# Moving the convolution, gate, factor and score steps of a four-part fp32 network on one core

## The chip, the cores and the metric

The kernel runs on one core of one Trainium2 chip. Its time is the device time of one execution in microseconds; a lower one is better. The engines are named as in the profile: PE is TensorE with PEld for its weight loads, DVE is VectorE, ACT is ScalarE, POOL is GpSimd, and SP is the queue that issues the transfers of the weights.

## The reference

Two blocks follow each other over one sequence of 256 tokens with 1024 features, all in fp32. The first block is a mixer of retention and latent attention with a SwiGLU network behind it. The second block has an even layer (spatial gate and stick-breaking attention), an MLP, an odd layer (mLSTM) and an MLP. The change touches a step of the retention, the even layer and the odd layer. Cut to these:

```
def _even_mixer(h, ...):
    ...
    q = _rmsnorm_2(zb[..., :B_WIDTH].reshape(bsz, seq, B_HEADS, B_HDIM), qn_g)
    k = _rmsnorm_2(zb[..., B_WIDTH:2 * B_WIDTH].reshape(bsz, seq, B_HEADS, B_HDIM), kn_g)
    ...
    o = _stick_breaking(to_bhsd(q), to_bhsd(k), to_bhsd(v))

def _odd_mixer(h, w_in, conv_w, conv_b, i_b, f_b, on_g, w_out):
    p = h @ w_in
    qk = jax.nn.silu(_causal_conv(p[..., :n_qk], conv_w, conv_b))   # four taps
    ...
    hc = _mlstm(q, k, v, i_pre, f_pre)

# _mlstm, by chunk: logf = log_sigmoid(f_pre); bcum = cumsum(logf)
dmat = where(tril, bcum[..., :, None] - bcum[..., None, :] + li[..., None, :], -inf)
m_t = maximum(g, max(dmat, -1))
wts = exp(dmat - m_t[..., None])
s = einsum('bhtd,bhsd->bhts', qc, kc) * wts
den = sum(s, -1) + inter * einsum('bhtd,bhd->bht', qc, n_st)
h = num / maximum(abs(den), exp(-m_t))[..., None]
```

## The kernel before, in words

Activations lie with features on the partitions and the 256 tokens along the free axis. Weights stream from memory in blocks of 128 x 1024 in the order of use. Each block is split into a high part H (rounded, by ScalarE, L368) and a rest L (by VectorE, L369), and each weight tile makes three TensorE products: high with high, high with low, low with high. They go into the PSUM tiles `st`; a product over feature tiles has 256 columns (`fm`, `fm2`), one over token tiles has 512 (`nat`). These are the stream products. All small products (sums over partitions, spreads of a row over partitions, transposes, scores, outputs) go into four PSUM tiles `sd` and are called side steps.

A side step is a closure. `side` puts steps in a list of which one is issued after each so many ticks (a tick is one weight tile of 128 columns); `plan` gives each step a fixed tick; `tick` issues what is due; `drain` issues all that is left. This sets the order in which the program is written. A scheduler then orders each engine's instructions by its own estimates, so a step can move a little against the stream; products issued with the last argument of `mm` true (`follow`) keep the written order among themselves, and a step wrapped in `urgent` has priority.

In the odd layer `qk_head(h)` takes head h's two halves (a query and a key tile). For each half it applies the four taps: ScalarE makes two products (L1295, L1296), GpSimd one product (L1297, tile `cvb`) and a sum (L1298, `cva`), VectorE a product with sum (L1299) and a sum (L1300); then tanh (L1302) and a last step into `qk` (L1303). `gate_chain` makes from the gate columns the rows B (running sum), `cc`, M (running maximum) and `em` = exp(-(B + M)) (L1321, L1322), whose minimum with 1e17 GpSimd takes (L1323). `gate_cols` turns `cc` and `em` into columns by four products of four columns each; `weights(h)`, `scores(h)` and `dens` use them.

In the even layer `project` makes queries, then keys. `head_sums` sums their squares by head, `head_factor` makes the factors (`faq` for queries, L1075 to L1082), and `q_scale` spreads `faq` over the partitions by 16 products and multiplies the queries (L1098). In the retention `outs(g)` makes the output of a pair of heads.

Of the kernel before, what the change touches and what calls it, by code (L numbers as in the profile page):

```python
# [11 lines left out]
ALU = mybir.AluOpType  # L12
# [4 lines left out]
T = 256  # L17
# [220 lines left out]
class K:  # L238
# [294 lines left out]
    def mixer1(s):  # L533
        nc, ap = s.nc, s.ap
# [225 lines left out]
        def outs(g):  # L760
            def f():
                Vc = Vcs[g]
                po = s.psd().rearrange("p (q h d) -> p q h d", q=2, h=2)
                for q in range(2):
                    for i in range(2):
                        for j, (t0, n) in enumerate(KT):
                            s.mm(po[:, q, i], Ss[g, j][:n, i, q * 128:q * 128 + 128], Vc[:n, i, j], j == 0, j == 2)
                oo = on[g // 2][:, :, (g % 2) * 256:(g % 2) * 256 + 256]
                nc.scalar.copy(oo, po.rearrange("p q h d -> p q (h d)"))
                vs = s.sm(4, "vs")  # L770
                jk = s.wk(T, "w256")[:, :128]
                for q in range(2):
                    for i in range(2):
                        nc.scalar.activation(jk, po[:, q, i], AF.Square, accum_out=vs[:, 2 * q + i:2 * q + i + 1])
                cb = comb[:, :, 2 * g:2 * g + 2]
                t = s.sm(4, "gnv")
                nc.vector.tensor_scalar(t, vs, 1.0 / 128, 1e-5, ALU.mult, ALU.add)
                nc.gpsimd.tensor_tensor(t, t, s.c("mhalf", 0, 4), ALU.pow)
                for q in range(2):
                    nc.vector.tensor_scalar(cb[:, q], t[:, 2 * q:2 * q + 2], r128[:, q:q + 1], 0.5, ALU.mult, ALU.mult)  # L780
                if g < 2:
                    decay(g + 2)
            return f

        for h in range(8):
            p = s.pst()[:, :NA]
            s.fm(("w_in",), 8, (p,), H, L)
            vt = s.wk(288, "P")
            nc.gpsimd.memset(vt[:, NA:], 0.0)
            nc.vector.tensor_mul(vt[:, :NA], p, rb)  # L790
            g, i = h // 2, h % 2
            s.side([center(g, i, vt)] + ([scores(g, 1), scores(g, 2), outs(g)] if i else [stack(g), scores(g, 0)]), 2)


        cH, cL = (lambda kt: ckvH[:, kt]), (lambda kt: ckvL[:, kt])
# [244 lines left out]
    def even(s):  # L1040
# [42 lines left out]
                                            0.125 if w == "q" else 1.0, ALU.mult, ALU.mult)  # L1083
            return f

        def q_scale(g):
            def f():
                fa = fac["q"]
                pb = s.psd().rearrange("p (f n) -> p f n", f=2)
                for i in range(2):  # L1090
                    t = 2 * g + i
                    for j in range(2):
                        for e in range(2):
                            col = fa[:, 8 * j + 2 * t + e:8 * j + 2 * t + e + 1]
                            s.mm(pb[64 * e:64 * e + 64, i, 128 * j:128 * j + 128], col.to_broadcast([128, 64]), s.c("eye"),
                                 True, True, True)
                q = qr[:, 2 * g:2 * g + 2]
                nc.vector.tensor_mul(q, q, pb)  # L1098
            return f


        yH = [s.slot(10, [128, 4, T], F32R), s.slot(11, [128, 4, T], F32R)]
# [103 lines left out]
        for q in range(2):  # L1206
# [12 lines left out]


        project("q", qr, "qg")
        s.side([s.urgent(head_sums("q")), s.urgent(head_factor("q")), s.urgent(lambda: (q_scale(0)(), q_scale(1)()))], 4)
        project("k", kT, "kg")
        s.drain()
        s.plan([(2, head_sums("k")), (6, s.urgent(head_factor("k"))), (7, st_scores(0)), (11, st_scores(1)),
                (16, spatial(0)), (20, spatial(1)), (34, st_suffix(0)), (36, st_scores(2)), (48, st_suffix(1)),
                (50, st_scores(3)), (64, st_suffix(2)), (77, st_suffix(3))])

        ug = s.slot(18, [128, 4, T])
        for g in range(2):  # L1230
# [9 lines left out]
        gate(1)  # L1240
        for q in range(2):
            nc.scalar.activation(V[:, q], ps[q], AF.Copy, scale=rr[:, q:q + 1])
        s.plan([(n, st_out(i)) for i, n in enumerate((72, 75, 80, 92))], s.ticks)
        y_h = lambda kt: yH[kt // 4][:, kt % 4]
        y_l = lambda kt: yL[kt // 4][:, kt % 4]
        s.residual("ev_w_out_2", 8, y_h, y_l, 1.0, "gp0", ahead=4)
# [19 lines left out]
    def odd(s):  # L1266
# [19 lines left out]
        def qk_head(h):  # L1286
            ps = s.fm2("od_w_in_2", 8, H, L)
            a = s.wk(2 * 259).rearrange("p (f n) -> p f n", f=2)
            nc.gpsimd.memset(a[:, :, 0:3], 0.0)
            nc.vector.tensor_mul(a[:, :, 3:], ps, s.b2(rb))  # L1290
            for i in range(2):
                f = h + 4 * i
                w = lambda t: s.v("cw", 4 * f + t)
                y, y1, y2 = s.wk(T, "w256"), s.wk(T, "cva"), s.wk(T, "cvb")
                nc.scalar.activation(y, a[:, i, 3:259], AF.Identity, bias=s.v("cb", f), scale=w(3))  # L1295
                nc.scalar.activation(y1, a[:, i, 0:T], AF.Copy, scale=w(0))  # L1296
                nc.gpsimd.tensor_scalar(y2, a[:, i, 1:T + 1], w(1), None, ALU.mult)  # L1297
                nc.gpsimd.tensor_add(y1, y1, y2)  # L1298
                nc.vector.scalar_tensor_tensor(y, a[:, i, 2:T + 2], w(2), y, ALU.mult, ALU.add)  # L1299
                nc.vector.tensor_add(y, y, y1)  # L1300
                th = s.wk(T, "w256")
                nc.scalar.activation(th, y, AF.Tanh, scale=0.5)  # L1302
                nc.vector.scalar_tensor_tensor(qk[i][:, h], th, 1.0, y, ALU.add, ALU.mult)  # L1303


        def gate_chain():
# [12 lines left out]
            nc.vector.tensor_tensor_scan(M, cc, f2, 0.0, ALU.max, ALU.max)  # L1319

            nc.vector.tensor_add(em, B, M)  # L1321
            nc.scalar.activation(em, em, AF.Exp, scale=-1.0)  # L1322
            nc.gpsimd.tensor_scalar(em, em, 1e17, None, ALU.min)  # L1323

        def gate_cols():
            pc = s.psd()
            for j in range(2):
                s.mm(pc[:, 4 * j:4 * j + 4], cc[:, 128 * j:128 * j + 128], s.c("sel4"), True, True)
                s.mm(pc[:, 8 + 4 * j:12 + 4 * j], em[:, 128 * j:128 * j + 128], s.c("sel4"), True, True)
            nc.vector.tensor_copy(ccol, pc[:, 0:16])  # L1330
            s.split(Mr[:, 0], Mr[:, 1], M)


        def weights(h):
            def f():
                w = wt[h // 2][:, h % 2]
                pb = s.psd()[:, :T]
                for i in range(2):
                    s.mm(pb, sel4r[:, h:h + 1].to_broadcast([128, 128]), Mr[:, i], i == 0, i == 1)
# [11 lines left out]
        def scores(h):  # L1351
            def f():
                w, S = wt[h // 2][:, h % 2], sw[h // 2][:, h % 2]
                p = s.psd()[:, :384]
                s.mm(p[:, 0:256], qk[1][:, h, 0:128], qk[0][:, h], True, True, h == 3)
# [4 lines left out]
        def wait():  # L1360
            pass

        def dens():

# [65 lines left out]
        p = s.pst()[:, :T]  # L1430
        s.cols4("od_w_in_2", p, "gm1", lambda kt: s.x[:, kt, NM:])
        nc.vector.tensor_mul(gs[:, 0], p, rb)
        s.side([gate_chain, gate_cols] + [weights(h) for h in range(4)] + [scores(0)], 5)
        for h in range(1, 4):
            qk_head(h)
            s.steps += [wait, wait, scores(h)] if h == 3 else [scores(h)]
        s.steps += [wait, dens]

        V = [s.slot(6, [128, 1024]), s.slot(7, [128, 1024])]
        for cch in range(2):  # L1440
# [68 lines left out]
```

## Time and profile before

| | |
|---|---|
| median of 3 runs | 1005.91 us (1005.79 to 1007.25) |
| the profiled execution's own time | 1006.0 us |
| its span | 1004.2 us |
| busy: PE, DVE, ACT, POOL | 992.4, 686.0, 567.6, 144.5 us |
| weight transfers | 172.90 MB by one queue, 57.1% of the DMA engines' time |

The span goes from the first to the last instruction. Busy times of PE come from products whose ends are modelled and overlap; the distance from start to start tells what one costs. A tile's name is the program's, without buffer numbers: `sd<-cst,faq` is a product into `sd` whose operands are a constant and `faq`.

### The profile page before, as it was taken

The numbers are of one execution on the slowest core, as the hardware profiler recorded it, in microseconds if no ns is written. First come the engines' busy times: TensorE is split into PE (matmuls) and PEld (weight loads), VectorE is DVE, ScalarE is ACT, GpSimd is POOL, SyncE is SP. The second block draws the span as 40 slices with busy tenths as digits, with TensorE's granted clock in tenths as the row PEclk, the third lists the DMA queues.
The fourth block names the chain that finished last, engine by engine and source line by source line (L and its number), as shares of the span: only waits on it lengthen the run. The fifth ranks groups of instructions, "written<-read, shape, count | busy, mean of one in ns | idle before, by whom it ended". The sixth has DMA issues, their size and how long they took to land.

```text
span 1004.2 us, 19944 instructions
## 1 busy us (share of the span) xinstructions
PE 992.4 (99%) x8214; PEld 955.1 (95%) x8214; DVE 686.0 (68%) x941; ACT 567.6 (57%) x840; POOL 144.5 (14%) x158
## 2 busy tenths in 40 slices
PE   9999999999999999999999999999989999999998
PEld 8998889999999999998889999999978999999998
DVE  6889687477776675669767767555585577665443
ACT  7796566445545554566756665444485565555432
POOL 1633100000111111447100000011171000000000
PEclk9999999999999999999999999999998999999999
DMA  8643553466666666674346666666654466666671
GB/s 337 190 131 101 153 160 109 129 193 191 191 199 192 193 193 200 204 226 148 119 121 186 189 193 193 190 196 197 187 151 142 114 187 191 198 195 190 204 207 53
DMA packets 49515, 176.73 MB, mean 176 GB/s; under 512 B 5456, under 2 KB 6736, under 8 KB 49424
## 3 DMA queue, kind: packets, MB, share of 16 engines
q1 hardware_dynamic: 47808, 172.90, 57.1%
q8 instruction: 64, 1.05, 0.5%
q0 software_dynamic: 368, 1.31, 0.4%
q10 hardware_dynamic: 1248, 1.25, 0.4%
q14 instruction: 27, 0.22, 0.1%
HBM read 174.39 MB, written 1.05 MB: 175 GB/s over the span
## 4 chain that ended last, share of the span: by engine, by line
PE 89%; DVE 3%; ACT 3%; POOL 2%; issue 1%; DMA 1%; SPq 0%; ACTq 0%; DVEq 0%; POOLq 0%
PE st L339 82%; PE sd L339 7%; DVE L L369 1%; ACT H L368 1%; PE sd L344 1%; POOL cvb L1297 1%; DMA raw<-in_wpack 1%; DVE e L757 0%; ACT w L704 0%; POOL cva L1298 0%; DVE comb L780 0%; ACT L1302 0%; DVE s L745 0%; POOL s L1218 0%; DVE vmean L725 0%
## 5 line engine op out<-in xcount | busy, mean ns | idle before, releaser
L369 DVE TENSOR_TENSOR L<-raw,H 128x1024 fp32r<-128x1024 f32 (+1 forms) x327 | 409.9, 1254 | 233.3 <-ACT H L368 231.5
L368 ACT CAST H<-raw 128x1024 fp32r<-128x1024 f32 (+1 forms) x327 | 341.8, 1047 | 350.4 <-PE st L339 266.4
L339 PE MATMUL st<-uH,H 128*128 128x256 f32 (+1 forms) x1384 | 385.7, 280 | 0.7 <-ACT H L368 0.7
L339 PE MATMUL st<-uL,H 128*128 128x256 f32 (+1 forms) x1384 | 383.8, 278 | 0.0
L339 PE MATMUL st<-uH,L 128*128 128x256 f32 (+1 forms) x1384 | 382.4, 278 | 0.6 <-DVE L L369 0.6
L339 PE MATMUL st<-s,H 128*128 128x256 f32 (+1 forms) x2004 | 343.1, 276 | 0.0
L339 PEld LDWEIGHTS st<-s,H 128*128 128x128 f32 x2004 | 301.9, 188 | 0.7 <-issue 0.5
L339 PE MATMUL st<-s,L 128*128 128x256 f32 (+1 forms) x1002 | 276.1, 276 | 0.0
L339 PEld LDWEIGHTS st<-uH,H 128*128 128x128 f32 x1384 | 259.7, 188 | 5.1 <-issue 2.4
L339 PEld LDWEIGHTS st<-uL,H 128*128 128x128 f32 x1384 | 259.9, 188 | 3.3 <-issue 2.4
L339 PEld LDWEIGHTS st<-uH,L 128*128 128x128 f32 x1384 | 258.8, 188 | 1.7 <-DVE L L369 1.0
L339 PEld LDWEIGHTS st<-s,L 128*128 128x128 f32 x1002 | 188.1, 188 | 0.2 <-issue 0.2
L339 PE MATMUL sd<-s,s 128*64 128x128 f32 (+10 forms) x280 | 46.4, 337 | 0.0
L339 PE MATMUL st<-H,uH 128*128 128x512 f32 x96 | 39.4, 410 | 0.0
L339 PE MATMUL st<-H,uL 128*128 128x512 f32 x96 | 39.4, 410 | 0.0
L339 PE MATMUL st<-L,uH 128*128 128x512 f32 x96 | 38.6, 402 | 0.0
L339 PEld LDWEIGHTS sd<-s,s 128*64 128x64 f32 (+7 forms) x280 | 30.9, 162 | 7.2 <-issue 1.5
L453 POOL TENSOR_TENSOR rstd<-rp,cst 128x2 f32<-128x2 f32 x4 | 4.7, 1179 | 209.2 <-DVE rp L452 209.2
L441 DVE TENSOR_TENSOR s<-w,s 128x512 fp32r<-128x512 f32 (+1 forms) x54 | 31.2, 580 | 0.0
L991 POOL TENSOR_TENSOR w<-w,w 128x256 f32<-128x256 f32 x22 | 16.6, 754 | 98.5 <-DVE w L990 98.5
L440 ACT CAST s<-w 128x512 fp32r<-128x512 f32 (+1 forms) x54 | 28.5, 531 | 1.1
L1258 DVE SCALAR_TENSOR_TENSOR w<-st,rb 128x512 f32<-128x512 f32 x32 | 21.8, 687 | 8.0 <-PE st L339 8.0
(282 smaller groups left out, 791.7 us busy)
## 6 DMA issues: line engine op xcount, KB each, us to landing
raw<-in_wpack SPq DMA_DIRECT2D x324, 512.0 KB, 4.0
s<-in_even POOLq DMA_DIRECT2D x2, 512.0 KB, 6.1
out_yT<-vx ACTq DMA_DIRECT2D x3, 256.0 KB, 4.9
vx<-in_vx SPq DMA_DIRECT2D x2, 272.0 KB, 5.0
s<-in_tabs SPq DMA_DIRECT2D x1, 544.0 KB, 9.5
s<-in_tabs SPq DMA_DIRECT2D x1, 448.0 KB, 8.9
cst<-in_cst SPq DMA_DIRECT2D x1, 447.5 KB, 8.2
vx<-in_vx SPq DMA_DIRECT2D x1, 408.0 KB, 7.1
```

Of the source, the lines that this page charges most:

```text
L339: i = s.nc.tensor.matmul(out, lhsT=l, rhs=r, start=start, stop=stop, skip_group_check=True)
L344: s.nc.tensor.transpose(out, a, s.c("eye", 0, n)[:n])
L368: nc.scalar.copy(H[:, c:d], raw[:, c:d])
L369: nc.vector.tensor_sub(L[:, c:d], raw[:, c:d], H[:, c:d].bitcast(F32))
L440: s.nc.scalar.copy(hi, src)
L441: s.nc.vector.tensor_sub(lo, src, hi.bitcast(F32))
L453: nc.gpsimd.tensor_tensor(out, t, s.c("mhalf", 0, n)[:out.shape[0]], ALU.pow)
L991: nc.gpsimd.tensor_mul(th, th, z[:, 1])
L1258: nc.vector.scalar_tensor_tensor(z, p, 0.0, s.b2(rb), ALU.max, ALU.mult)
L1297: nc.gpsimd.tensor_scalar(y2, a[:, i, 1:T + 1], w(1), None, ALU.mult)
```

## The change

Five things change. In the retention, an empty step is put ahead of `outs(g)`, and its products are issued with `follow`. In the even layer the steps for queries and keys get one plan with fixed ticks, counted from the start of the key projection, where before there was a list for the queries, a `drain` behind the keys, and a plan for the rest; `q_scale` becomes one step for all four tiles, at tick 37, and the four output steps get ticks that are 32 higher, since the count no longer starts anew. In the odd layer's convolution GpSimd's product goes to VectorE as a product with sum, and GpSimd makes the last sum in place of VectorE. The minimum on `em` goes from GpSimd to VectorE. The gate, weight and score steps get fixed ticks, and more of their products are issued with `follow`.

```diff
-            s.side([center(g, i, vt)] + ([scores(g, 1), scores(g, 2), outs(g)] if i else [stack(g), scores(g, 0)]), 2)
+            s.side([center(g, i, vt)] + ([scores(g, 1), scores(g, 2), lambda: None, outs(g)] if i else [stack(g), scores(g, 0)]), 2)
...
         project("q", qr, "qg")
-        s.side([s.urgent(head_sums("q")), s.urgent(head_factor("q")), s.urgent(lambda: (q_scale(0)(), q_scale(1)()))], 4)
+        s.plan([(1, s.urgent(head_sums("q"))), (3, s.urgent(head_factor("q"))), (34, head_sums("k")), (37, q_scale),
+                (39, s.urgent(head_factor("k"))), (40, st_scores(0)), (43, st_scores(1)), (48, spatial(0)), (52, spatial(1)),
+                (66, st_suffix(0)), (68, st_scores(2)), (80, st_suffix(1)), (82, st_scores(3)), (96, st_suffix(2)),
+                (109, st_suffix(3))])
         project("k", kT, "kg")
-        s.drain()
-        s.plan([(2, head_sums("k")), (6, s.urgent(head_factor("k"))), (7, st_scores(0)), (11, st_scores(1)),
...
-        s.plan([(n, st_out(i)) for i, n in enumerate((72, 75, 80, 92))], s.ticks)
+        s.plan([(n, st_out(i)) for i, n in enumerate((104, 107, 112, 124))], s.ticks)
...
-                nc.gpsimd.tensor_scalar(y2, a[:, i, 1:T + 1], w(1), None, ALU.mult)
-                nc.gpsimd.tensor_add(y1, y1, y2)
                 nc.vector.scalar_tensor_tensor(y, a[:, i, 2:T + 2], w(2), y, ALU.mult, ALU.add)
-                nc.vector.tensor_add(y, y, y1)
+                nc.vector.scalar_tensor_tensor(y1, a[:, i, 1:T + 1], w(1), y1, ALU.mult, ALU.add)
+                nc.gpsimd.tensor_add(y, y, y1)
...
-            nc.gpsimd.tensor_scalar(em, em, 1e17, None, ALU.min)
+            nc.vector.tensor_scalar_min(em, em, 1e17)
...
-        s.side([gate_chain, gate_cols] + [weights(h) for h in range(4)] + [scores(0)], 5)
+        s.plan([(2, s.urgent(gate_chain)), (40, gate_cols)] + [(43 + 3 * h, weights(h)) for h in range(4)] +
+               [(56 + 4 * h, scores(h)) for h in range(3)] + [(70, scores(3)), (77, dens)])
         for h in range(1, 4):
             qk_head(h)
-            s.steps += [wait, wait, scores(h)] if h == 3 else [scores(h)]
-        s.steps += [wait, dens]
```

What the scheduler makes of it is seen at three places. The first is VectorE in the odd layer, from the sum B + M (L1321 before, L1317 now) on. `s_8667` and `s_8668` hold the gate rows, `w_...` the halves of the convolution, `s_8671` the remainder of the split of M. Before:

```order
L1321 TENSOR_TENSOR s_8668<-s_8667,s_8668 128x256
L369 TENSOR_TENSOR L<-raw,H 128x1024
L441 TENSOR_TENSOR s_8671<-s_8668,s_8671 128x256
L1303 SCALAR_TENSOR_TENSOR s_8659<-w_9005,w_8996 128x256
L1299 SCALAR_TENSOR_TENSOR w_9008<-w_8993,vx,w_9008 128x256
```

And now:

```order
L1317 TENSOR_TENSOR s_8668<-s_8667,s_8668 128x256
L441 TENSOR_TENSOR s_8671<-s_8668,s_8671 128x256
L369 TENSOR_TENSOR L<-raw,H 128x1024
L1299 SCALAR_TENSOR_TENSOR s_8659<-w_8963,w_8956 128x256
L1294 SCALAR_TENSOR_TENSOR w_8966<-w_8953,vx,w_8966 128x256
L1295 SCALAR_TENSOR_TENSOR cva<-w_9057,vx,cva 128x256
L1319 TENSOR_SCALAR s_8668<-s_8668 128x256
```

The minimum (L1319 now) stands sixth behind the sum; on GpSimd it stood between the sums and products of the convolution. (By the changed file's lines, L1299 is the old L1303, L1294 the old L1299, and L1295 is the new step.)

The second place is TensorE in the odd layer, from the second group of `weights` products (`sd<-s_8671,s_8672`) to the three gate columns that need `em` or come with it (`128x4`). Before:

```order
L339 MATMUL sd<-s_8671,s_8672 128x256 x3
L339 MATMUL st<-H,uH 128x512
L339 MATMUL st<-H,uL 128x512
L339 MATMUL st<-L,uH 128x512
L339 MATMUL st<-H,uH 128x512
L339 MATMUL sd<-cst,s_8668 128x4
L339 MATMUL sd<-cst,s_8667 128x4
```

And now, with six stream products of the same three kinds more, left out here:

```order
L339 MATMUL sd<-s_8671,s_8672 128x256 x3
L339 MATMUL st<-H,uH 128x512
...
L339 MATMUL st<-L,uH 128x512
L339 MATMUL st<-H,uH 128x512
L339 MATMUL sd<-cst,s_8668 128x4
L339 MATMUL sd<-cst,s_8667 128x4
```

Ten stream products stand there in place of four, and three more ahead of the first row, so the gate columns come nine stream products later.

The third place is TensorE in the even layer, at the spread of the query factors (`faq`) and the sums of the keys' squares (`sd<-s_5462,cst`). Before:

```order
L339 MATMUL st<-uL,H 128x256
L339 MATMUL st<-uH,L 128x256
L339 MATMUL sd<-cst,faq 64x128 x16
L339 MATMUL sd<-s_5462,cst 32x256 x4
L339 MATMUL st<-uH,H 128x256
```

And now, with nine stream products left out behind the first row:

```order
L339 MATMUL sd<-s_5462,cst 32x256 x2
...
L339 MATMUL sd<-cst,faq 64x128 x13
L339 MATMUL sd<-s_5462,cst 32x256 x2
L339 MATMUL sd<-cst,faq 64x128 x3
L339 MATMUL st<-uH,H 128x256
```

Two of the four sums moved ahead of the spread, and three stream products behind it; the spread is cut by the other two sums.

## Rows read from the trace of the kernel before

**Rows 1.** The page: busy time by engine; granted TensorE clock in 40 slices, in tenths.

```profile
PE 992.4 (99%) x8214; PEld 955.1 (95%) x8214; DVE 686.0 (68%) x941; ACT 567.6 (57%) x840; POOL 144.5 (14%) x158
...
PEclk9999999999999999999999999999998999999999
```

**Rows 2.** Who TensorE waited for: us in total, times, longest us.

```profile
PE sd L339 <- POOL s L1323: 3.3, 1, 3.3
PE sd L339 <- DVE faq L1082: 1.5, 1, 1.5
```

**Rows 3.** Windows: length, busy us (x instructions) by engine, granted clock, DMA share, GB/s.

```profile
727.90:749.70 21.80, 21.80 (x153) 18.85 (x151) 18.35 (x30) 18.79 (x31) 16.04 (x10) 1.00 0.45 136
...
753.10:758.80 5.70, 5.68 (x16) 4.75 (x17) 4.37 (x11) 3.10 (x6) 2.97 (x3) 0.50 0.48 158
```

**Rows 4.** Timeline, TensorE, 739 to 770: start us, us, engine, line, operation, out<-in, count.

```profile
739.15 0.39 PE L339 MATMUL st<-L,uH 128*128 128x512 f32 x1
...
743.12 0.39 PE L339 MATMUL st<-H,uL 128*128 128x512 f32 x1
743.35 0.28 PE L339 MATMUL sd<-cst,s 128*128 128x4 f32 x2
743.49 0.48 PE L339 MATMUL st<-L,uH 128*128 128x512 f32 x1
743.80 0.40 PE L339 MATMUL st<-H,uH 128*128 128x512 f32 x1
...
749.47 0.40 PE L339 MATMUL st<-H,uH 128*128 128x512 f32 x1
753.12 1.44 PE L339 MATMUL sd<-cst,s 128*128 128x4 f32 x6 [3.26 <-POOL s L1323]
...
758.81 0.39 PE L339 MATMUL st<-L,uH 128*128 128x512 f32 x1
...
769.20 0.81 PE L339 MATMUL sd<-s,s 128*128 128x256 f32 x4
```

**Rows 5.** Timeline, GpSimd, 743 to 753.

```profile
743.46 4.81 POOL L1297 TENSOR_SCALAR cvb<-w,vx 128x256 f32<-128x256 f32 x1
...
749.92 2.20 POOL L1297 TENSOR_SCALAR cvb<-w,vx 128x256 f32<-128x256 f32 x1
752.21 0.86 POOL L1323 TENSOR_SCALAR s<-s 128x256 f32<-128x256 f32 x1
```

**Rows 6.** Groups by line, 725 to 765: busy us, mean ns; idle before and releaser.

```profile
L1297 POOL TENSOR_SCALAR cvb<-w,vx 128x256 f32<-128x256 f32 x8 | 15.7, 1956 | 5.5 <-DVE w L1290 4.8
...
L1298 POOL TENSOR_TENSOR cva<-cva,cvb 128x256 f32<-128x256 f32 x8 | 7.6, 954 | 6.2 <-DVE w L1299 4.4 <-ACT cva L1296 1.5
...
L1299 DVE SCALAR_TENSOR_TENSOR w<-w,vx,w 128x256 f32<-128x256 f32 x8 | 4.5, 559 | 0.5 <-ACT w L1295 0.3
```

**Rows 7.** Timelines, VectorE and ScalarE, 745 to 765.

```profile
745.33 0.42 DVE L1321 TENSOR_TENSOR s<-s,s 128x256 f32<-128x256 f32 x1
...
746.80 0.42 DVE L441 TENSOR_TENSOR s<-s,s 128x256 fp32r<-128x256 f32 x1
...
764.30 0.42 DVE L1303 SCALAR_TENSOR_TENSOR s<-w,w 128x256 f32<-128x256 f32 x1
...
746.47 0.41 ACT L1322 ACTIVATE s<-s 128x256 f32<-128x256 f32 x1
```

**Rows 8.** Timeline, TensorE, 473 to 478.

```profile
473.37 0.28 PE L339 MATMUL st<-uH,L 128*128 128x256 f32 x1
475.18 1.97 PE L339 MATMUL sd<-cst,faq 128*64 128x128 f32 x32 [1.54 <-DVE faq L1082]
477.08 0.64 PE L339 MATMUL sd<-s,cst 128*32 128x256 f32 x8
```

**Rows 9.** Line L1082 (ns min/median/max, starts) and GpSimd's timeline at 473.

```profile
L1082 DVE TENSOR_SCALAR faq<-faq,rr x2: 219/724/1229, 473.9 to 475.0; 128x8 f32<-128x8 f32 x2
...
472.90 2.21 POOL L1218 TENSOR_TENSOR s<-e,s 128x512 f32<-128x512 f32 x1
```

More of the change, by code (lines that the diff above doesn't have):

```diff
@@ L766, in f @@
                         for j, (t0, n) in enumerate(KT):
-                            s.mm(po[:, q, i], Ss[g, j][:n, i, q * 128:q * 128 + 128], Vc[:n, i, j], j == 0, j == 2)
+                            s.mm(po[:, q, i], Ss[g, j][:n, i, q * 128:q * 128 + 128], Vc[:n, i, j], j == 0, j == 2, True)
                 oo = on[g // 2][:, :, (g % 2) * 256:(g % 2) * 256 + 256]
@@ L1084, in head_factor, with q_scale @@
             return f
[L1086 to L1096, printed above, removed]
+        def q_scale():
+            fa = fac["q"]
+            pb = [s.psd().rearrange("p (f n) -> p f n", f=2) for _ in range(2)]
+            for t in range(4):
+                for j in range(2):
+                    for e in range(2):
+                        col = fa[:, 8 * j + 2 * t + e:8 * j + 2 * t + e + 1]
+                        s.mm(pb[t // 2][64 * e:64 * e + 64, t % 2, 128 * j:128 * j + 128], col.to_broadcast([128, 64]),
+                             s.c("eye"), True, True, True)
+            for g in range(2):
                 q = qr[:, 2 * g:2 * g + 2]
-                nc.vector.tensor_mul(q, q, pb)
-            return f
+                nc.vector.tensor_mul(q, q, pb[g])
         yH = [s.slot(10, [128, 4, T], F32R), s.slot(11, [128, 4, T], F32R)]
@@ L1221, in even @@
         project("q", qr, "qg")
-        s.side([s.urgent(head_sums("q")), s.urgent(head_factor("q")), s.urgent(lambda: (q_scale(0)(), q_scale(1)()))], 4)
+        s.plan([(1, s.urgent(head_sums("q"))), (3, s.urgent(head_factor("q"))), (34, head_sums("k")), (37, q_scale),
+                (39, s.urgent(head_factor("k"))), (40, st_scores(0)), (43, st_scores(1)), (48, spatial(0)), (52, spatial(1)),
+                (66, st_suffix(0)), (68, st_scores(2)), (80, st_suffix(1)), (82, st_scores(3)), (96, st_suffix(2)),
+                (109, st_suffix(3))])
         project("k", kT, "kg")
-        s.drain()
-        s.plan([(2, head_sums("k")), (6, s.urgent(head_factor("k"))), (7, st_scores(0)), (11, st_scores(1)),
-                (16, spatial(0)), (20, spatial(1)), (34, st_suffix(0)), (36, st_scores(2)), (48, st_suffix(1)),
-                (50, st_scores(3)), (64, st_suffix(2)), (77, st_suffix(3))])
         ug = s.slot(18, [128, 4, T])
@@ L1293, in qk_head @@
                 w = lambda t: s.v("cw", 4 * f + t)
-                y, y1, y2 = s.wk(T, "w256"), s.wk(T, "cva"), s.wk(T, "cvb")
+                y, y1 = s.wk(T, "w256"), s.wk(T, ("cva", "cvb")[i])
                 nc.scalar.activation(y, a[:, i, 3:259], AF.Identity, bias=s.v("cb", f), scale=w(3))
                 nc.scalar.activation(y1, a[:, i, 0:T], AF.Copy, scale=w(0))
-                nc.gpsimd.tensor_scalar(y2, a[:, i, 1:T + 1], w(1), None, ALU.mult)
-                nc.gpsimd.tensor_add(y1, y1, y2)
                 nc.vector.scalar_tensor_tensor(y, a[:, i, 2:T + 2], w(2), y, ALU.mult, ALU.add)
-                nc.vector.tensor_add(y, y, y1)
+                nc.vector.scalar_tensor_tensor(y1, a[:, i, 1:T + 1], w(1), y1, ALU.mult, ALU.add)
+                nc.gpsimd.tensor_add(y, y, y1)
                 th = s.wk(T, "w256")
@@ L1327, in gate_cols @@
             for j in range(2):
-                s.mm(pc[:, 4 * j:4 * j + 4], cc[:, 128 * j:128 * j + 128], s.c("sel4"), True, True)
+                s.mm(pc[:, 4 * j:4 * j + 4], cc[:, 128 * j:128 * j + 128], s.c("sel4"), True, True, True)
                 s.mm(pc[:, 8 + 4 * j:12 + 4 * j], em[:, 128 * j:128 * j + 128], s.c("sel4"), True, True)
@@ L1338, in f @@
                 for i in range(2):
-                    s.mm(pb, sel4r[:, h:h + 1].to_broadcast([128, 128]), Mr[:, i], i == 0, i == 1)
+                    s.mm(pb, sel4r[:, h:h + 1].to_broadcast([128, 128]), Mr[:, i], i == 0, i == 1, True)
                 nc.vector.scalar_tensor_tensor(w[:, 0:256], pb, ccol[:, h:h + 1], s.c("mask0", 1, 257), ALU.add, ALU.min)
@@ L1354, in f @@
                 p = s.psd()[:, :384]
-                s.mm(p[:, 0:256], qk[1][:, h, 0:128], qk[0][:, h], True, True, h == 3)
+                s.mm(p[:, 0:256], qk[1][:, h, 0:128], qk[0][:, h], True, True, True)
                 s.mm(p[:, 256:384], qk[1][:, h, 128:256], qk[0][:, h, 128:256], True, True)
@@ L1358, in scores @@
             return f
-        def wait():
-            pass
         def dens():
```

## The prediction

> **What bounds the kernel now.** I read the page first. TensorE is busy 99% of the span, and its granted clock is full in all slices but one [rows 1]. So the work of the other engines costs time only where TensorE waits for it, and the whole change moves work between or on those engines: its number of TensorE products stays as it is. Next I asked who TensorE waits for. Two waits stand in the code that the change touches [rows 2]: 3.3 us for the minimum that GpSimd takes of the gate row `em` (L1323), and 1.5 us for the query factors `faq` of VectorE (L1082). The other rows of that view are in the first 100 us or around a weight block, in code whose order the change leaves alone. Then I looked at each wait in order of time.
>
> The first is in the mLSTM layer. The products with four columns that `gate_cols` makes are in two places: one at 743.35, and three more at 753.12, which need `em` [rows 4]. Before those the array is empty from 749.87 on. GpSimd shows why: `em`'s exponential is done by ScalarE at 746.88 [rows 7], but GpSimd is then in a convolution product (L1297) that takes 4.81 us, does the sum behind it and another product of 2.20 us, and takes the minimum only at 752.21 to 753.07 [rows 5]. TensorE starts 0.05 us later. What follows is the second half of the loss: from 753.1 to 758.8 the granted clock is 0.50, that is 1.2 in place of 2.4 GHz [rows 3], after 3.25 us in which the array did nothing. The other wait, of 1.54 us at 475.18 [rows 8], has no clock loss behind it: the slices of the page there are full.
>
> **The change part by part, and the sum.** *The wait for `em`.* From the start of the last product before it (749.47) to the first one at full speed again (758.81) 9.34 us pass [rows 4]. In them are 11 stream products of 512 columns (the one at 749.47 and ten behind the gate columns) and three gate-column products. At full clock a stream product costs 0.2335 us (739.15 to 743.12 are 17 of them). One gate-column product costs 0.14 to the next start and 0.07 on the stream product behind it (743.35, 743.49, 743.80, where two stream steps would take 0.47 and 0.68 pass from 743.12 to 743.80). So the full price is 11 x 0.2335 + 3 x 0.14 + 0.07 = 3.06 us, and 9.34 - 3.06 = 6.28 us is what goes if nothing waits there and the clock stays up.
>
> Does `em` come in time? In the changed order the minimum is VectorE's: five instructions stand between the sum `B + M` and it, the copy's remainder, an L (L369), a last step of a convolution (L1303) and the two steps of the next half. The sum starts at 745.33 in the trace; it and one L take 1.47 us, up to the start of the remainder at 746.80 [rows 7]. Then come the remainder and the L1303 step, 0.42 us each at most (the length of the remainder's row), and two three-operand steps at 0.56 each, the mean of L1299 [rows 6]. A minimum over 256 columns has no row for VectorE. It is bounded by the 0.86 us that GpSimd took [rows 5] and the 0.22 us of VectorE's shortest scalar step [rows 9]; I take 0.42, its sum over as many columns. Together 745.33 + 1.47 + 0.84 + 1.12 + 0.42 = 749.2. One more L may come ahead of the sum (1.47 - 0.42 = 1.05 us): 750.2. TensorE asks for it later than before: six stream products more stand between the weight products and the three gate columns, and three more ahead of those, so it is there at 749.47 + 10 x 0.2335 = 751.8. The margin is 1.6 to 2.6 us.
>
> *The convolution.* Of its two GpSimd steps per half, the product goes to VectorE's three-operand step (0.56 us [rows 6] in place of a sum of 0.42 there, eight times: 1.1 us more) and one sum stays on GpSimd: of 15.7 + 7.6 us of GpSimd's work [rows 6] some 7.6 are left. This lies beside TensorE, at a cost of nothing, covered by VectorE's idle time: 18.35 us busy of 21.80 [rows 3]. With the cover gone each microsecond of lag in the L steps would be one of TensorE's. What is late next is the scores of head 3, which need the last convolution: TensorE is there at 769.20 now [rows 4], so 769.20 - 6.28, less two stream products, 762.4 then; the last convolution step starts at 764.30 now [rows 7]. But it starts that late because of the wait in question: it is the end of a chain of halves, each of which waited for GpSimd. Without that the chain of the two last halves should be some 5 us sooner. I take no wait, bounds 0 and 764.72 - 762.4 = 2.3 us.
>
> *The rule that speaks against it.* In the even layer a step of VectorE over 16 columns ended only when GpSimd's sum did: its first `faq` step, 1.23 us long, where the second took 0.22 [rows 9]. The Trainium skill (SBUF — State Buffer, "Who interferes with whom") has that as a rule: VectorE's scalar steps, and its steps with two inputs in SBUF, exclude a GpSimd step that reads SBUF, and who starts second waits for the whole of the other. By this the minimum could stand behind one convolution sum. With the 0.95 us that such a sum takes here, the mean of L1298 [rows 6], `em` is there by 751.2; by the rule the sum stays the same, but the margin falls to 0.6 us.
>
> *The query factors.* The change means the spread of the factors (`q_scale`) to come later and the factors sooner. In the order it does little: on VectorE, ScalarE and GpSimd the instructions of this stretch keep their order, and on TensorE two of the four sums over the keys go ahead of the spread, and three stream products behind it. The factors are ready when the blocked `faq` step ends with GpSimd's L1218 at 475.11 [rows 9], and nothing in the change moves that. So TensorE still starts the spread at about 475.18. Behind it are two sums less (half of the 0.64 us at 477.08) and three stream products of 256 columns more (half of 0.2335 each, 0.35 us): nothing. The bounds are -1.7 us, the whole gap from 473.37 + 0.12 to 475.18 [rows 8], and +0.3 us, the price of the two sums without cover.
>
> *The rest.* The retention step that is put one later, and its products that are now kept in order, move no instruction on any engine: 0. The stick-breaking outputs get numbers higher by 32, but the count that they are compared with no longer restarts: same place, 0. The new fixed numbers of the weight and score steps move them by at most a few stream products: no work is added.
>
> Sum against the profiled execution's own 1006.0 us (its span is 1004.2, so 1.8 lie around it; the median of the runs shown is 1005.91): 1006.0 - 6.28 = 999.7 us, 0.6% faster. About 0.2%, 2 us, is what a measurement can tell from no change.
>
> **The rivals.** *The even wait goes as well* (5%): if the factors come before TensorE does, up to 1.54 us more are won: 998.2. For it speaks that a block between VectorE and GpSimd depends on which starts first; against it the unchanged order of both.
>
> *A shorter wait takes its place* (11%): the scores of head 3 or the gate columns wait up to 2.3 us. The wait of 1.54 us left the clock alone, so the price is the wait itself: 1000.7 to 1002.0. Against it are the margins above.
>
> *The change doesn't do what it says* (7%): `em` is still late by over 3 us and the clock falls again, 1004 to 1006, because the minimum stands behind a VectorE step (L1303) that waits for ScalarE, which waits for a GpSimd sum. For it: VectorE runs in order, and two more of its steps than before hang on GpSimd. Against: TensorE comes 2.1 us later, and GpSimd has half its work.
>
> *Slower* (5%): the GpSimd sums block VectorE. Each now stands between two VectorE steps of the same half. Some five of the eight fall into the stretch of 21.80 us in which VectorE has 3.45 us free (half of the ten GpSimd steps there [rows 3]). If each held VectorE for as long as a GpSimd product took on average (1.96 us [rows 6]), that is 9.8 us, 6.35 over what is free, and TensorE would wait for L by that. The clock would fall as it did; that part was 6.28 - 3.42 = 2.9 us (the start moved from 749.70 to 753.12). So 999.7 + 6.35 + 2.9 = 1009.0. It decides from 0.7 us per sum on (3.45 / 5), and the kernel is slower than before from 1.4 on. Against it: the same form of sum (L1298) ran eight times here, VectorE's share holds what it blocked, and TensorE did not wait for L in this stretch.
>
> **How the numbers follow.** The forecast has 72% with a range of its own from 999.0 to 1000.7 (the even bound of +0.3, and part of the spread of runs, 1005.79 to 1007.25). Faster by over 0.2% are the forecast, the even wait and the shorter wait: 0.88. Within 0.2%: 0.07. Slower: 0.05. The range that should hold 8 in 10 goes from 998.2, with the even wait gone, to 1002.6, past the shorter wait at its bound.
>
> **What would show it.** Right: no wait of TensorE for `em`, the granted clock at 1.00 in all slices around 750 us, the minimum on VectorE ending between 748.5 and 751, and the gate columns at about 751.8. The wait for `faq` stays, at 1.0 to 1.6 us, and starts of the spread at 475.2. GpSimd's busy time falls by some 16 us without effect elsewhere. Wrong: TensorE waiting for L or for the last convolution in 740 to 765, a clock under 1.00 there, or a wait for `faq` that is gone.

## The result and the profile after

| | before | changed kernel |
|---|---|---|
| median of 6 runs | 1005.91 us (1005.79 to 1007.25) | 1001.33 us (1000.54 to 1001.84) |
| profiled execution, its span | 1006.0, 1004.2 us | 1001.84, 1000.1 us |

The ratio of the runs is 0.995, 95% interval 0.9938 to 0.9963. The change gains 4.6 us where 6.2 were forecast (1005.91 to 999.7). To find the missing 1.6 us, I cut both traces at the same three places: where TensorE's stream goes to 512 columns in the even layer, where it does so in the odd layer, and where it goes back to 256 columns behind that. These are the products that start there, in the timeline of TensorE, before:

```profile
434.69 0.42 PE L339 MATMUL st<-H,uH 128*128 128x512 f32 x1
...
738.65 0.42 PE L339 MATMUL st<-H,uH 128*128 128x512 f32 x1
...
771.71 0.28 PE L339 MATMUL st<-uH,H 128*128 128x256 f32 x1
```

And in the changed kernel:

```profile
435.65 0.42 PE L339 MATMUL st<-H,uH 128*128 128x512 f32 x1
...
740.30 0.42 PE L339 MATMUL st<-H,uH 128*128 128x512 f32 x1
...
767.57 0.28 PE L339 MATMUL st<-uH,H 128*128 128x256 f32 x1
```

The part up to the first place is 0.96 us longer, the even part (304.65 us where it was 303.96) 0.69 us longer, and the odd part (27.27 us where it was 33.06) 5.79 us shorter. Together that is -4.14, the difference of the spans within 0.1 us; what follows is alike.

In the odd layer the main of the forecast came true. The wait for `em` is gone from TensorE's waits, the wait for `faq` is shorter but there (1.1 for 1.5 us in [rows 2]), and the clock is full in all slices [rows 1]. Page and waits of the changed kernel:

```profile
PE 992.4 (99%) x8214; PEld 955.6 (96%) x8214; DVE 688.5 (69%) x942; ACT 567.1 (57%) x840; POOL 130.9 (13%) x149
...
PEclk9999999999999999999999999999999999999999
```

```profile
PE sd L339 <- DVE faq L1082: 1.1, 1, 1.1
```

In the window that answers to the half-speed one of [rows 3] the granted clock (the number behind the five engines) is 1.00:

```profile
753.20:757.20 4.00, 3.94 (x20) 3.03 (x19) 3.98 (x6) 3.71 (x8) 1.17 (x2) 1.00 0.41 138
```

But the margin that I had worked out was used up. TensorE, around the gate columns [rows 4]:

```profile
753.21 0.40 PE L339 MATMUL st<-H,uH 128*128 128x512 f32 x1
753.66 0.83 PE L339 MATMUL sd<-cst,s 128*128 128x4 f32 x6
754.35 0.48 PE L339 MATMUL st<-H,uL 128*128 128x512 f32 x1
```

A stream product costs 0.23 us, so the columns could have started at 753.44: they wait 0.2 us. The reason stands in the timelines of GpSimd, VectorE and ScalarE (rows of [rows 5, 7] before):

```profile
747.14 3.87 POOL L1296 TENSOR_TENSOR w<-w,cva 128x256 f32<-128x256 f32 x1 [5.18 <-DVE w L1294]
752.54 0.91 POOL L1296 TENSOR_TENSOR w<-w,cvb 128x256 f32<-128x256 f32 x1 [1.54 <-DVE w L1294]
```

```profile
747.38 1.21 DVE L369 TENSOR_TENSOR L<-raw,H 128x1024 fp32r<-128x1024 f32 x1
748.51 0.41 DVE L1317 TENSOR_TENSOR s<-s,s 128x256 f32<-128x256 f32 x1
748.85 0.41 DVE L441 TENSOR_TENSOR s<-s,s 128x256 fp32r<-128x256 f32 x1
749.18 1.21 DVE L369 TENSOR_TENSOR L<-raw,H 128x1024 fp32r<-128x1024 f32 x1
751.48 0.43 DVE L1299 SCALAR_TENSOR_TENSOR s<-w,w 128x256 f32<-128x256 f32 x1 [1.09 <-ACT w L1298]
751.98 0.48 DVE L1294 SCALAR_TENSOR_TENSOR w<-w,vx,w 128x256 f32<-128x256 f32 x1
752.38 0.48 DVE L1295 SCALAR_TENSOR_TENSOR cva<-w,vx,cva 128x256 f32<-128x256 f32 x1
752.78 0.83 DVE L1319 TENSOR_SCALAR s<-s 128x256 f32<-128x256 f32 x1
```

```profile
751.03 0.42 ACT L1298 ACTIVATE w<-w 128x256 f32<-128x256 f32 x1 [2.96 <-POOL w L1296]
...
752.25 0.40 ACT L1318 ACTIVATE s<-s 128x256 f32<-128x256 f32 x1
```

Read them from top to bottom. GpSimd's sum starts at 747.14 and ends at 751.01, 0.6 us after VectorE's four steps in a row (each with two operands in SBUF) have ended at 750.39. The tanh (L1298) waits for the sum, and `em`'s exponential (L1318), which stood ahead of that tanh before, now stands behind it on ScalarE. So it runs at 752.25 only and ends at 752.65. VectorE itself waits for the same tanh, 1.09 us ahead of L1299, and has two more steps to do before the minimum. The minimum follows them at 752.78, without a wait of its own, and takes 0.83 us beside the next GpSimd sum (752.54 to 753.45). So one late sum holds up both ways to the minimum, and of the two VectorE's queue ended last, by 0.1 us.

In the even layer the rows that answer to [rows 8] show what became of the spread:

```profile
472.97 0.28 PE L339 MATMUL st<-uH,L 128*128 128x256 f32 x1
473.18 0.62 PE L339 MATMUL sd<-s,cst 128*32 128x256 f32 x4
473.73 0.39 PE L339 MATMUL st<-uH,H 128*128 128x256 f32 x1
...
474.78 0.28 PE L339 MATMUL st<-uH,L 128*128 128x256 f32 x1
476.13 1.74 PE L339 MATMUL sd<-cst,faq 128*64 128x128 f32 x26 [1.07 <-DVE faq L1082]
477.81 0.63 PE L339 MATMUL sd<-s,cst 128*32 128x256 f32 x4
478.36 0.65 PE L339 MATMUL sd<-cst,faq 128*64 128x128 f32 x6
478.94 0.39 PE L339 MATMUL st<-uH,H 128*128 128x256 f32 x1
```

The spread and two sums now take 2.81 us (476.13 to 478.94). Before, the spread and four sums took 2.47 (475.18 to the next stream product at 477.65). The two sums that went ahead cost about 0.76 us there (473.18 to 473.95, less one stream step of 0.11, and 0.1 before them). Less empty time of the array (1.24 for 1.69 us) gives 0.45 back: 0.34 + 0.76 - 0.45 = 0.65 us lost.

The first 0.96 us are lost in the start, in instructions that stand in the same order in both kernels. Products of 256 columns there, before:

```profile
6.41 0.28 PE L339 MATMUL st<-uH,H 128*128 128x256 f32 x1
6.53 0.28 PE L339 MATMUL st<-uL,H 128*128 128x256 f32 x1
```

And in the changed kernel:

```profile
7.46 0.41 PE L339 MATMUL st<-uH,H 128*128 128x256 f32 x1
7.67 0.41 PE L339 MATMUL st<-uL,H 128*128 128x256 f32 x1
```

They come 0.21 us apart instead of 0.12, up to 10.3. Whether that is the change's doing is for the experiments.

### The profile page after: what moved, and what is told of

It reads as the page before. It is cut to its first block, busy times and chain, and to the rows that moved or that the text cites. A ratio compares the mean times of both kernels' runs of the same rounds, so it can differ in the third digit from the quotient of the medians.

```text
span 1000.1 us, 19921 instructions
## 1 busy us (share of the span) xinstructions
PE 992.4 (99%) x8214; PEld 955.6 (96%) x8214; DVE 688.5 (69%) x942; ACT 567.1 (57%) x840; POOL 130.9 (13%) x149
## 3 DMA queue, kind: packets, MB, share of 16 engines
q8 instruction: 64, 1.05, 0.4%
HBM read 174.39 MB, written 1.05 MB: 175 GB/s over the span
## 4 chain that ended last, share of the span: by engine, by line
PE 91%; DVE 3%; ACT 3%; issue 1%; POOL 1%; DMA 0%; ACTq 0%; POOLq 0%
PE st L339 84%; PE sd L339 7%; DVE L L369 1%; PE sd L344 1%; ACT H L368 1%; DVE e L757 0%; POOL w L1296 0%; ACT w L704 0%; DMA vx<-in_vx 0%; DVE comb L780 0%; DVE s L745 0%; ACT w L1292 0%; POOL s L1216 0%; DVE vmean L725 0%; ACT s L697 0%
```

## The experiments

Seven kernels, each against the kernel before on the same chip (its median was 1006.14 us beside runs 1 to 4 and 1006.62 beside 5 to 7), so that kernels are compared by the ratio. The table has the three stages of each profiled run, cut as above, in us.

| kernel | up to the even layer | even | odd | median us | ratio to before, 95% |
|---|---|---|---|---|---|
| before | 434.69 | 303.96 | 33.06 | 1005.91 | |
| changed | 435.65 | 304.65 | 27.27 | 1001.33 | 0.9950 (0.9938 to 0.9963) |
| 1 minimum only | 434.85 | 303.99 | 26.96 | 1000.11 | 0.9939 (0.9927 to 0.9952) |
| 2 convolution only | 434.26 | 303.99 | 30.22 | 1002.97 | 0.9969 (0.9958 to 0.9980) |
| 3 even layer only | 434.74 | 304.63 | 33.06 | 1006.91 | 1.0008 (0.9999 to 1.0017) |
| 4 without even layer | 435.83 | 303.98 | 27.64 | 1001.10 | 0.9948 (0.9934 to 0.9961) |
| 5 minimum, late spread | 435.62 | 302.65 | 26.96 | 998.98 | 0.9925 (0.9912 to 0.9939) |
| 6 sum on VectorE | 435.65 | 304.63 | 26.96 | 1001.43 | 0.9948 (0.9936 to 0.9961) |
| 7 no gain on GpSimd | 434.57 | 303.51 | 27.64 | 1000.00 | 0.9935 (0.9923 to 0.9948) |

Two things are read from it first. The even and odd stages repeat to 0.03 us where the code is the same, with one exception: the odd stage of the changed kernel takes 27.27 us in its own trace and 27.64 in those of runs 4 and 7, which have the same code there (run 4 shows the place). So a difference of 0.3 us in a stage counts where the rows show its place, though the median of a kernel's runs moves by as much. And the start has two levels, 434.3 to 434.9 and 435.6 to 435.8, in kernels whose first 400 us are the same (5 has the start of the kernel before and is late, 7 that of the changed kernel and is not).

**1. The minimum only.**

```diff
-            nc.gpsimd.tensor_scalar(em, em, 1e17, None, ALU.min)
+            nc.vector.tensor_scalar_min(em, em, 1e17)
```

> The kernel before, with the minimum of em on VectorE and nothing else changed. Theory A (the minimum's engine is the whole odd gain): VectorE has the minimum behind the L at 748.02, so em is there at about 749.6; TensorE asks for it four stream products later than before, at about 750.6, does not wait, the granted clock stays at 1.00, and the odd stage (from the first 512-column product to the first 256-column one behind it, 33.06 us before, 27.27 in the changed kernel) is about 27.0 us; the time is about 1000 us. Theory B (the convolution's products on GpSimd would make the next wait): the halves still go through GpSimd one after the other, the last one ends at about 763.4, and TensorE waits for the scores of head 3 from 762.4 on, by 1 to 2.3 us: odd stage 28 to 29.5 us, time 1000.7 to 1002. The wait for the query factors stays as before at 1.5 us.

Theory A holds. In its timeline the minimum, TensorE's gate columns, the last step of the convolution and the scores of head 3 stand like this:

```profile
749.33 0.82 DVE L1323 TENSOR_SCALAR s<-s 128x256 f32<-128x256 f32 x1
...
759.59 0.41 DVE L1303 SCALAR_TENSOR_TENSOR s<-w,w 128x256 f32<-128x256 f32 x1
```

```profile
750.82 0.73 PE L339 MATMUL sd<-cst,s 128*128 128x4 f32 x6
751.40 0.48 PE L339 MATMUL st<-L,uH 128*128 128x512 f32 x1
...
763.28 0.81 PE L339 MATMUL sd<-s,s 128*128 128x256 f32 x4
```

`em` is there 0.67 us before TensorE wants it, and the last convolution 3.3 us before its scores, with all of GpSimd's products and sums where they were. One line gives 6.10 us of the odd stage; the convolution on GpSimd is no limit once `em` does not stand behind it.

**2. The convolution only** (the minimum stays on GpSimd).

```diff
...
-                nc.gpsimd.tensor_scalar(y2, a[:, i, 1:T + 1], w(1), None, ALU.mult)
-                nc.gpsimd.tensor_add(y1, y1, y2)
...
-                nc.vector.tensor_add(y, y, y1)
+                nc.vector.scalar_tensor_tensor(y1, a[:, i, 1:T + 1], w(1), y1, ALU.mult, ALU.add)
+                nc.gpsimd.tensor_add(y, y, y1)
```

> The kernel before, with only the convolution changed (product to VectorE, last sum on GpSimd); the minimum stays on GpSimd. If GpSimd's product of 4.81 us was what kept em late, em's minimum is free to run as soon as the exponential is done, and the wait is under 1 us: odd stage about 27.5 us, time about 1000. If, as the trace of the changed kernel suggests, the sum on GpSimd that stands behind back-to-back VectorE steps (3.87 us there) takes the product's place, then tanh, and behind it on ScalarE the exponential of em, come at about 751 to 752, the minimum at about 752.5 to 753.5, TensorE asks at 749.7 and waits 2.5 to 3.5 us; with a clock that falls as before the odd stage is 31 to 33 us and the time 1004 to 1006; without the fall 30 us and 1003.

The second theory holds in kind, with a shorter wait: I had not taken off that this run is 2.05 us ahead of the changed kernel's trace. GpSimd, TensorE, and the window behind the wait:

```profile
745.09 3.86 POOL L1299 TENSOR_TENSOR w<-w,cva 128x256 f32<-128x256 f32 x1 [5.18 <-DVE w L1297]
750.69 0.87 POOL L1322 TENSOR_SCALAR s<-s 128x256 f32<-128x256 f32 x1 [1.74 <-ACT s L1321]
```

```profile
749.77 0.40 PE L339 MATMUL st<-H,uH 128*128 128x512 f32 x1
751.61 0.83 PE L339 MATMUL sd<-cst,s 128*128 128x4 f32 x6 [1.45 <-POOL s L1322]
```

```profile
752.60:756.00 3.40, 3.40 (x9) 2.64 (x8) 3.31 (x5) 3.24 (x7) 0.73 (x1) 0.51 0.48 135
```

The held-up sum is there again (3.86 us). The array is empty for 1.6 us, and then the granted clock is 0.51, the lower level, for more than 3 us. The odd stage is 3.26 us longer than in run 1, twice the empty time. Against the kernel before, the convolution on its own gains 2.84 us.

**3. The even layer only, and 4. the changed kernel without it.** The edit is the even layer's part of the diff, put into the kernel before, and taken out of the changed one.

> The kernel before, with only the even layer changed (one plan with fixed ticks, spread of the query factors and sums of the keys at ticks 37 and 34, outputs' ticks 32 higher). Theory A (the cut spread costs the time): the part from the first 256-column product of the even layer to the next 512-column one is 45.48 us as in the changed kernel, against 44.80 before, the wait for faq 1.07 instead of 1.54, and the time 0.7 us longer than before, 1006.6. Theory B (the 0.7 us in the changed kernel are a variation between runs, or come from the retention): 44.8 us and 1005.9.

> The changed kernel with the even layer as before; the retention, the convolution, the minimum and the ticks of the odd layer stay changed. Theory A: 44.8 us in the even part instead of 45.48, odd stage 27.3 us as in the changed kernel, time 0.7 us under the changed kernel's median of 1001.33, 1000.6. Theory B: the even part still takes 45.5 us and the time stays at 1001.3. The start (first 5 to 10 us, where the profiled run of the changed kernel took 0.21 us a product for 5 us instead of 0.117 and lost 0.96 us in code that is the same) differs from run to run in both.

Theory A holds in the stages: 304.63 with the new plan, 303.98 without it. In run 3 TensorE does what it did in the changed kernel, with the spread cut by two sums (the wait in the bracket is the same 1.07 us):

```profile
475.22 1.74 PE L339 MATMUL sd<-cst,faq 128*64 128x128 f32 x26 [1.07 <-DVE faq L1082]
476.89 0.63 PE L339 MATMUL sd<-s,cst 128*32 128x256 f32 x4
477.45 0.65 PE L339 MATMUL sd<-cst,faq 128*64 128x128 f32 x6
```

The medians say it less well: 1006.91 against 1006.14, with an interval that just holds no change, and run 4 is not under the changed kernel by the 0.7 us (a ratio of 0.9948 for 0.9950; its profiled start was long, and its odd stage is 27.64). That stage has the changed kernel's code and is still 0.37 longer. Its trace has a sum on GpSimd that took 2.04 us where the changed kernel's took 0.91, and TensorE is idle for 0.2 us ahead of the third group of weight products. Below are that sum, VectorE's L beside it, the L at the same place in the changed kernel's trace, and TensorE in run 4:

```profile
755.17 2.04 POOL L1299 TENSOR_TENSOR w<-w,cva 128x256 f32<-128x256 f32 x1 [2.20 <-DVE w L1297]
```

```profile
755.40 1.22 DVE L369 TENSOR_TENSOR L<-raw,H 128x1024 fp32r<-128x1024 f32 x1
```

```profile
755.89 1.76 DVE L369 TENSOR_TENSOR L<-raw,H 128x1024 fp32r<-128x1024 f32 x1
```

```profile
758.39 0.40 PE L339 MATMUL st<-L,uH 128*128 128x512 f32 x1
758.82 0.50 PE L339 MATMUL sd<-s,s 128*128 128x256 f32 x2
```

In the changed kernel the sum went first and the L took 1.76 us; in run 4, and the same way in run 7, the L went first and the sum took 2.04. In all three the sum starts 0.16 to 0.17 us into the VectorE step ahead of the L. What decides between them is open.

**5. The minimum, and the spread later and uncut.** The kernel before with the minimum as in run 1, `q_scale` as one step, and this plan (shown against the changed kernel's):

```diff
-        s.plan([(1, ...), (3, ...), (34, head_sums("k")), (37, q_scale),
-                (39, s.urgent(head_factor("k"))), (40, st_scores(0)), (43, st_scores(1)), (48, spatial(0)), (52, spatial(1)),
+        s.plan([(1, ...), (3, ...), (43, q_scale), (44, head_sums("k")),
+                (48, s.urgent(head_factor("k"))), (49, st_scores(0)), (52, st_scores(1)), (56, spatial(0)), (60, spatial(1)),
```

> The kernel before with two things: the minimum of em on VectorE, and in the even layer one step for the spread of the query factors that is issued 15 stream products later than before (tick 43, sums of the keys behind it at 44, key factors 48, scores 49 and 52, spatial steps 56 and 60, the rest as in the changed kernel's plan). The convolution stays as before. Theory A (the factors' time is set by GpSimd's sums, so TensorE only has to come later, and the spread must not be cut): 15 products of 0.113 us cover the 1.69 us in which the array is empty, the wait for faq is at most 0.1 us, the even part takes 43.1 to 43.4 us (44.83 less 1.55), the odd stage 27.0 us, and the time is 998.5 us, below both kernels. Rival: the key factors and scores, 5 to 10 ticks later, become late in their turn, and 0.5 to 1.5 us of it come back as a wait for fak or for the first scores: 999 to 1000.

Theory A holds in kind, with less gained: the part that was to take 43.1 to 43.4 us takes 43.79, 1.04 us under run 1's 44.83 in place of 1.55. The even stage as a whole is 1.34 us under run 1's; the other 0.3 us come behind that part and were not expected. The spread stands in one piece, with no wait, and the sums in one piece behind it:

```profile
476.20 1.97 PE L339 MATMUL sd<-cst,faq 128*64 128x128 f32 x32
478.64 0.64 PE L339 MATMUL sd<-s,cst 128*32 128x256 f32 x8
```

Three stream products now stand between them, so the stream is interrupted twice instead of once. By TensorE's starts (0.20 us from the last stream product to the spread and to the sums, 0.22 from the first stream product behind the spread to the next, where 0.11 is usual) that makes some 0.3 of the 0.5 us missing in that part; the rest no run tells apart. TensorE waits for nothing in turn. At 998.98 us, 0.75% under the kernel before, this version has the lowest ratio of all, though its interval still meets run 1's.

**6. The convolution's last sum on VectorE.**

```diff
-                nc.gpsimd.tensor_add(y, y, y1)
+                nc.vector.tensor_add(y, y, y1)
```

> The changed kernel, but the convolution's last sum stands on VectorE again, so GpSimd has no part in the convolution. Theory A (a GpSimd sum of 3.87 us, held up by VectorE's steps one behind the other, delays tanh, the exponential of em and the column copy): the exponential is done by 750, the minimum by about 751, there is no wait at the gate columns, none of 0.2 us at the last weight products, and the odd stage takes 26.9 to 27.0 us as with the minimum alone, against 27.27 and 27.64 in the two runs with the GpSimd sums: time 1000.8 to 1001.0. Theory B (VectorE's three-operand steps are what costs): VectorE has eight sums of 0.42 us more, its lag grows, and the odd stage takes 27.5 to 29 us: 1001.5 to 1003.

The odd stage decides for theory A: 26.96 us, as with the minimum alone, although VectorE has eight sums more to do. The minimum ends 11.54 us after the start of the stage, where it ended 13.31 after it in the changed kernel, and no step of the convolution waits for GpSimd. (The order of TensorE differs too: the gate columns come four stream products later than in the changed kernel. But `em` would be in time without them.) The minimum has no GpSimd step beside it and takes 0.28 us:

```profile
751.54 0.28 DVE L1319 TENSOR_SCALAR s<-s 128x256 f32<-128x256 f32 x1
```

The 0.31 us gained on the changed kernel do not show in the ratio (0.9948 for 0.9950).

**7. No gain on GpSimd.**

```diff
...
-            nc.gpsimd.tensor_mul(z, z, lng[:, 0])
-            nc.gpsimd.tensor_add(vg[:, q], z, lng[:, 1])
+            if q == 0:
+                nc.gpsimd.tensor_mul(z, z, lng[:, 0])
+                nc.gpsimd.tensor_add(vg[:, q], z, lng[:, 1])
```

> The changed kernel without the two GpSimd steps on the second half of the normalised gate values (its gain and its shift are left out there; the first half keeps them). Theory A (what makes the query factors late is GpSimd's sum of 2.21 us, which holds up VectorE's first faq step): that step takes 0.22 instead of 1.23 us, the factors are ready about 1.3 to 1.8 us sooner, before TensorE comes, the wait of 1.07 us is gone, the even part takes 44.2 to 44.5 us instead of 45.48 and the time is about 1000.3 us. Theory B (the factors come late because of the L ahead of them on VectorE, whose raw block or H is late): the wait stays at about 1 us and the time at 1001.3.

Theory A holds. VectorE's two `faq` steps take 0.36 us together (1.37 in the changed kernel), TensorE waits for nothing there, and the even stage is 1.14 us shorter than the changed kernel's:

```profile
473.09 0.36 DVE L1082 TENSOR_SCALAR faq<-faq,rr 128x8 f32<-128x8 f32 x2
```

So the time of the factors was GpSimd's to set, as read from [rows 9], and no step of the change touches that.

## Why the prediction was right, and where it was not

The measured 1001.33 us lie within the range of 998.2 to 1002.6, but above the 999.0 to 1000.7 of the forecast itself. They lie where the rival "a shorter wait takes its place" was put, and not for its reason: the gate columns wait 0.2 us, the scores of head 3 not at all. So the direction and the largest term are right by their mechanism. That the range held the result is in part luck, since room left for one rival took in two terms that were set at nothing.

**The wait for `em` and the clock: right in mechanism and size.** 6.28 us were forecast. Run 1, which does this and nothing else, gains 6.10. The 0.18 less is nearly all the price of the gate columns: the three together take 0.58 us in run 1 (750.82 to 751.40), and three times 0.14 was taken. Both halves are real: the wait, and the stretch at the lower clock behind it.

**When `em` is ready: wrong by about 2 us.** The step said 749.2 to 750.2, and 751.2 at worst. The minimum ended at 753.61; less the 1.65 us by which this trace is behind at the start of the odd layer (740.30 for 738.65) that is 751.96. The sign that it ends between 748.5 and 751 failed with it. I had added up VectorE's steps as if none waited, and taken the exponential as done early, because it was done at 746.88 before. In the new order both stand behind one tanh that waits for a GpSimd sum. VectorE's L1299 (the old L1303) waits 1.09 us for it, and the exponential comes behind it on ScalarE and is done 0.13 us before the minimum starts. The sum B + M also starts later than I took it (748.51 less 1.65 is 746.86, for 745.33; of this 1.53 us the upper bound had 1.05), and the minimum takes 0.83 us for 0.42. Run 6 shows that it was the GpSimd sum: without it the minimum ends 11.54 us after the start of the stage, within the 10.55 to 11.55 that 749.2 to 750.2 come to. I had given this chain 7% under "doesn't do what it says", with VectorE's L1303 step as its place. That is what happened, but it made `em` late by 0.2 us for TensorE and not by over 3. It used up the margin of 1.6 to 2.6 us and 0.2 more. The wait stayed at 0.2 us since TensorE has nine stream products more before it asks, which is 2.1 us. That part of the step was right: TensorE could have started the columns at 753.44, less 1.65 that is 751.79, and 751.8 was forecast. With the old list of steps run 1 has four products more and run 2 three; how much of the nine the new ticks make was not tried alone.

The rule that I cited (the Trainium skill, SBUF — State Buffer, "Who interferes with whom") is borne out where I used it: beside a GpSimd sum the minimum takes 0.83 us, without one 0.28. I left out the other direction. There the trace goes past the rule as I had put it: the sum that came second was held not for one VectorE step but for four in a row, 3.87 us in place of the 0.7 to 0.9 of a sum that is not held up, in each of four traces (changed, 2, 4, 7: 3.86 or 3.87). It is not so at every meeting, as run 4 shows. The kernel before had the same thing, as far as its timelines go: the product of 4.81 us that kept `em` late there [rows 5] stood beside six such VectorE steps in a row (743.88 to 747.56), and the shortest of its kind took 0.94. So the change put a held-up sum where a held-up product had been. GpSimd's busy time fell by 13.6 us where some 16 were expected; the held-up sum counts as busy.

**The convolution: taken at nothing, costs 0.3 to 0.7 us.** The bounds were 0 and 2.3, with the scores of head 3 as the place. Those never waited. The step that failed is "covered by VectorE's idle time": it counted VectorE's free time, and not how long VectorE's steps can hold up the one sum that stays on GpSimd. Against run 1 the changed kernel's odd stage is 0.31 longer and that of runs 4 and 7 0.68. The 0.31 are the 0.2 us of wait at the gate columns and 0.1 in the columns themselves (0.69 us, 753.66 to 754.35, for 0.58 in run 1). Run 6 takes the GpSimd sum out and is at 26.96 again, so it is the sum that costs, through the late gate columns and, in 4 and 7, the late weight products. The same comparison says that the convolution part of the change gains nothing beside the minimum: with the minimum on VectorE, GpSimd had time for its products.

**The query factors: taken at nothing, cost 0.69 us (0.65 between runs 3 and 4).** The upper bound, +0.3, was too low. The step that failed is the price of nothing for two sums less and three stream products more behind the spread. It counted products, and left out that small products are dearer in pieces: two sums ahead interrupt the stream once more, and two sums in the middle cut the spread. I had taken half of 0.64 us for two sums; alone they take 0.55 (473.18 to 473.73), where four in a piece took 0.57 (477.08 to 477.65), and the stream loses 0.1 us before and 0.1 behind them. Runs 3 and 4 show the size, and run 5 that the uncut spread, put 15 products later, takes the wait with it. That `faq` itself would come no sooner was right (run 3; run 7 shows what it would have taken). By [rows 9] each `faq` step has 8 columns, not the 16 that the prediction says; nothing hangs on that.

**The retention and the outputs' ticks.** Forecast at nothing, since the order of the instructions stays. They were not tried alone; runs 4 and 6, which hold them, show nothing that would be theirs.

**A rival's price.** That a shorter wait costs "the wait itself" was wrong for the odd layer: in run 2 an empty array of 1.6 us was followed by more than 3 us at the lower clock. Behind the 1.69 us empty in the even layer [rows 8] it was 1.00; removing them gave 1.04 us there (run 5). What makes the difference is open.

**The sum.** -6.10, + 0.31, + 0.69 make -5.1 us. The profiled pair shows -4.14, because its start was 0.96 us longer, which comes and goes with the run. So of the 1.6 us missing about 1.2 are shown to be the change's (0.31 and 0.69 over what I took, and 0.18 of the first term); the rest is within the spread of the runs and the start.

## What to carry to other kernels

When an instruction moves to another engine, follow its input and every step ahead of it in the new queue: the new order may have put them behind a wait that was not there before. Do one part of a change at a time: here one line gives all of the gain, and the two parts beside it cost about 1 us. To hide a wait whose end is fixed, put the waiting products later in one piece; pieces cost more than their count suggests.

## What was not expected of the hardware

- A GpSimd sum over 256 columns took 3.87 us when VectorE issued four steps with two SBUF operands one behind the other, and ended 0.6 us after the last of them, in four traces; 0.71 to 0.92 us was usual. At another place of the same code the sum went first in one trace (0.91 us, and the VectorE step behind it took 1.76 for 1.22) and last in two (2.04 us).
- Pauses of TensorE of the same length (1.6 and 1.69 us) were followed by a granted clock of 0.51 in one place (run 2) and 1.00 in another (even layer of the kernel before).
- In the first 12 us some executions have 10 or 11 steps of about 0.21 us from one TensorE entry to the next (changed kernel, 4, 5, 6), others 1 to 4 (before, 1, 2, 3, 7), while the granted clock is shown as 1.00 there. In the odd layer of the kernel before 512 columns took 0.43 us at a granted clock of 0.50, twice as much for twice the columns; what the clock was in the start these records do not settle. The first group is the one that comes late to the even layer (435.6 to 435.8 for 434.3 to 434.9).
